# The last level of the block inverses in a hybrid decoder layer: 64 by 64 products in quarters of the TensorE array, in bundles of eight, in place of full operands with zeros

## The chip, the cores and the metric

The kernel runs on one core of a Trainium2 chip. The metric is the device time of one execution in microseconds (us). The kernel before took 1600.16 us (median of three runs, 1599.25 to 1602.24). One execution was also recorded by the hardware profiler; that one took 1599.81 us, and its span from the first to the last instruction is 1597.8 us. The engines are named as the profile names them: PE is TensorE's matmul side and PEld its weight loads, DVE is VectorE, ACT is ScalarE, POOL is GpSimd and SP is SyncE, which here only issues transfers.

## The reference

One decoder layer over 1024 positions of width 2048, followed by a final RMSNorm. An input projection feeds three groups of heads: a chunked spatial gating, a gated DeltaNet of 8 heads, and a cross-attention into 256 memory tokens. Their gated outputs go through one output projection. What the change touches is the inverse inside the DeltaNet, which the reference computes chunk by chunk with a triangular solve:

```python
    a = jnp.where(strict, jnp.einsum('bhnid,bhnjd->bhnij', kb, k) * decay, 0.0)
    eye = jnp.eye(C, dtype=f32)
    T = lax.linalg.triangular_solve(a + eye, jnp.broadcast_to(eye, a.shape),
                                    left_side=True, lower=True, unit_diagonal=True)
    value = jnp.einsum('bhnij,bhnjd->bhnid', T, vb)
    k_cumdecay = jnp.einsum('bhnij,bhnjd->bhnid', T, kb * jnp.exp(g_cum)[..., None])
```

## The kernel before

**The large products.** The input and output projections take most of the time. They are float32 products made of three TensorE products each: every operand is split into a high part and the rest (`ahi`, `alo`, `whi`, `wlo`, also `zh`, `zl`), and `triple` multiplies high by high, high by low and low by high. `seven` runs a block scheme with seven products per pair of column blocks (a pass of Strassen's kind), in sub-products with a 128 by 128 stationary operand and 512 moving columns. These appear in the profile as `acc<-ahi,whi 128*128 128x512` and the like; below they are called the main products.

**The DeltaNet beside them.** It works on chunks of 128 positions, for two heads and 512 positions at a time: eight chunk matrices, in the free dimension of one tile. `front` makes the products of keys and queries (through `qk`, whose `to_tokens` transposes eight blocks in a row), `inverse` inverts the 32 by 32 diagonal blocks on DVE, `levels` makes the inverse of each 128 by 128 matrix out of these, `values` prepares the values, and `back` runs the recurrence (`scan_step`) and the output (`heads_out`, again with eight transposes in a row). `backs` calls `front_late`, `levels`, `values` and `back` eight times in all, each for a pair of heads and a half of the sequence; in the profiled execution these calls lie between 720 and 1100 us.

**`levels` in steps.** Tile `gt` holds the eight matrices (views `ge`, `go`: even and odd chunks), `tblk` (`t`, `te`, `to`) the blocks of the inverse, `ut` (`u`, `ue`, `uo`) its transpose, which is the result. The diagonal blocks are fetched by transfers on POOL's queue. The first level goes from 32 to 64 with products of 32 by 32 in separate sub-arrays (`32*32` in the profile): a bundle of 16 products, copies to `y1` by ACT, a bundle of 24 products, copies by ACT. The last level goes from 64 to 128 and needs two products per chunk, each 64 by 64 by 64. In the kernel before, two chunks share one full operand: the block of the even chunk lies in `ge[0:64, :, 64:128]`, that of the odd chunk was copied by a transfer to `ge[64:128, :, 0:64]`, so that both stand on the counter-diagonal of a 128 by 128 stationary operand, and two memsets on DVE set its diagonal quarters to zero. One matmul with 64 moving columns then gives the product of the even chunk in output partitions 64 to 127 and that of the odd chunk in 0 to 63. There are four such matmuls for the eight chunks (`dn<-tblk,gt 128x64` in the profile), then two copies by ACT to the diagonally placed tile `z` (which is `y2`, set to zero once by POOL at the start), then four more matmuls (`dn<-ut,y 128x64`) and two copies to `ut`. A float32 matmul stands in the profile as two records of weights and two of products, so each group of four is eight records.

**What sets the order.** Nothing is issued as the code is read. `Plan.add` records every operation with its dependencies, `Plan.issue` plans all engines with costs in nanoseconds (`price`) and then issues everything in the order of the planned times. Of the operations that could start on an engine the one with the lowest `rank` goes first; main products have rank 9, so whatever else PE can do goes between them. An operation of PE that waits for another engine is planned at least `SLACK` (600 ns) after the planned end of what it waits for, within `levels` 800 ns more (`R.slow`). Operations recorded under `together()` become one bundle: they wait for everything that any of them needs and stand next to each other. After a bundle of more than eight operations (`len(head.tail) > 7`) the plan adds `SWITCH` (250 ns) to PE's clock. Matmuls outside a bundle are planned one by one, so other work can come between them. A float32 matmul is priced in `price` like this:

```python
            passes = 1 if ins[0].dtype == F32R else 2 if name == "transpose" else 4
            o.cost = max(13.3 + n / 2.4 * passes, 222.0 if passes == 4 else 110.0) if out.shape[0] == P else max(30.0, n / 2.4 * passes * out.shape[0] / P)
```

All instructions bear the profile's line L300, where the plan issues them, so they are told apart by their tiles.

Of the kernel before, what the change touches and what calls it, by code (L numbers as in the profile page):

```python
# [17 lines left out]
P = 128  # L18
# [42 lines left out]
class Plan:  # L61
# [27 lines left out]
    @contextmanager  # L89
    def rank(self, cls):  # L90
        old, self.cls = self.cls, cls
        yield
        self.cls = old
# [135 lines left out]
    def issue(self):  # L229
        free = dict.fromkeys(self.SEEN, 0.0)  # L230
        soon = {e: [] for e in free}
        now = {e: [] for e in free}
        held = {"dve": 0.0, "pool": 0.0}
        dma = 0.0
        beside = dict.fromkeys(free, 0.0)
        table = "exp"
        for o in self.ops:
            if o.n == 0 and o.lead is o:
                heapq.heappush(soon[o.eng], (0.0, o.idx))
        left = len(self.ops)  # L240
        while left:
            best = None
            for e in free:
                if now[e]:
                    t = free[e]
                elif soon[e]:
                    t = max(free[e], soon[e][0][0])
                else:
                    continue
                if best is None or t < best[0]:  # L250
                    best = (t, e)
            t, e = best
            while soon[e] and soon[e][0][0] <= t:
                i = heapq.heappop(soon[e])[1]
                heapq.heappush(now[e], (self.ops[i].cls, i))
            if e == "act":
                other = [(c + self.STAY * (self.ops[i].table not in (None, table)), i, c) for c, i in now[e]]
                _, i, c = min(other)
                now[e].remove((c, i))
                heapq.heapify(now[e])  # L260
                head = self.ops[i]
            else:
                head = self.ops[heapq.heappop(now[e])[1]]
            for o in (head, *head.tail):
                t = max(t, free[e])
                if o.table not in (None, table):
                    t, table = t + self.TABLE_LOAD, o.table
                o.at = t
                left -= 1
                if o.lock:  # L270
                    t = max(t, held["pool" if e == "dve" else "dve"])
                end = t + o.cost
                if o.lock:
                    held[e] = end
                free[e] = end - min(self.OVERLAP[e], 0.5 * o.cost)
                done = end + o.lat
                if o.moves:
                    dma = max(dma, end) + o.moves
                    beside[e] = max(beside[e], end) + 2 * o.moves
                    done = (dma if e == "sp" else max(dma, beside[e])) + self.DMA_FIXED + o.lat  # L280
                for s in o.succ:
                    if s.eng != e or o.moves:
                        when = done + self.SEEN[s.eng] + (self.SLACK if s.eng == "pe" else 0.0)
                    elif e == "pe":
                        when = free[e]
                    else:
                        when = end + 34.0
                    if o.moves or s.eng == "pe" != e:
                        when += s.late
                    if o.moves and s.eng == "pe":  # L290
                        when += o.land
                    s.ready = max(s.ready, when)
                    s.n -= 1
                    if s.n == 0:
                        heapq.heappush(soon[s.eng], (s.ready, s.idx))
            if len(head.tail) > 7:
                free[e] += self.SWITCH
        self.ops.sort(key=lambda o: (o.at, o.idx))
        for o in self.ops:
            o.fn(*o.args, **o.kw)  # L300
# [3 lines left out]
def kernel(  # L304
# [28 lines left out]
    R = Plan(nc)  # L333
    V, S, G, PE, Q = R.dve, R.act, R.pool, R.pe, R.sp
    rank, behind = R.rank, R.behind

    def C(shape, name, dt=F32):
        return sb.tile(list(shape), dt, name=name, tag=name)[:]
# [65 lines left out]
    ring = {t: Slots(t, 4, [P, HT]) for t in ("kT", "qT", "vs", "kd", "ai")}  # L404
# [19 lines left out]
    def tpb():  # L424
        turn["tp"] += 1
        return acc[2 + turn["tp"] % 2]
# [284 lines left out]
    tblk = C([P, 2 * NT, 64], "tblk")  # L711
# [81 lines left out]
    y2 = C([P, 2 * NT, 64], "y2")  # L793
# [240 lines left out]
    def levels(gt, tdr, udr):  # L1034


        NB = 2 * NT
# [7 lines left out]
        ut = ring["ut"]().rearrange("p (h t i) -> p h t i", h=2, i=P)  # L1045
        t, u = tblk, ut.rearrange("p h t i -> p (h t) i")
# [21 lines left out]
        d = work()  # L1068
# [6 lines left out]
        for b in (0, 64):  # L1075
            with rank(1):
                S.copy(y1[b + 32 : b + 64], d32[b + 32 : b + 64])
        with rank(1):
            V.memset(ge[0:64, :, 0:64], 0.0)
            V.memset(ge[64:P, :, 64:P], 0.0)  # L1080
        du = work()
        d32 = du[:, 0 : NB * 32].rearrange("p (c m) -> p c m", m=32)
        de, do = twos(d32)
        with R.together():
            for c in range(NB):
                for b in (0, 64):
                    PE.matmul(d32[b : b + 32, c], y1[b + 32 : b + 64, c], u[b + 32 : b + 64, c, b + 32 : b + 64],
                              start=True, stop=True)
                b = c % 2 * 64 + 32
# [9 lines left out]
                S.copy(u[b : b + 32, :, b + 32 : b + 64], d32[b : b + 32])  # L1099
        z = y2.rearrange("p (q e) m -> p q (e m)", e=2)  # L1100
        d = work()[:, 0 : NB * 32].rearrange("p (q m) -> p q m", m=64)
        for q in range(NB // 2):
            PE.matmul(d[:, q], ge[:, q], te[:, q], start=True, stop=True)
        with rank(1):
            S.copy(z[64:P, :, 0:64], d[64:P])
        with rank(1):
            S.copy(z[0:64, :, 64:P], d[0:64])
        d = work()[:, 0 : NB * 32].rearrange("p (q m) -> p q m", m=64)
        for q in range(NB // 2):
            PE.matmul(d[:, q], z[:, q], ue[:, q, 64:P], start=True, stop=True)  # L1110
        with rank(1):
            S.copy(ue[0:64, :, 64:P], d[0:64])
        with rank(1):
# [134 lines left out]
    a = tpb()  # L1248
# [29 lines left out]
    a = tpb()  # L1278
# [216 lines left out]
    def backs(ps, inv):  # L1495
        for hf in range(2):
            for p in ps:
                state = front_late(p, hf, inv[hf * 2 + p % 2])
                ut = levels(state[2], *state[-1])
                values(*state)  # L1500
                back(*state, ut)
# [9 lines left out]
    with rank(2.6):  # L1511
        gdrs += [front(1, hf) for hf in range(2)]
        early_inv = inverse([gdrs[i] for i in (0, 2, 1, 3)], "early", 1.9)
    for u in (y2, tblk, *ring["ut"].bufs):
        G.memset(u, 0.0)
    blocks(0, to_conv(0), to_conv(1))
    with rank(2.6):
# [313 lines left out]
```

## Time and profile before

| | |
|---|---|
| runs, median (lowest to highest) | 1600.16 us (1599.25 to 1602.24) |
| profiled execution, own time | 1599.81 us |
| its span, first to last instruction | 1597.8 us |
| granted TensorE clock | 0.999 |
| instructions | 26025 |

The span is cut into stages by looking at which tiles PE works on: up to some 110 us the memory's keys and values and the first half's rows, from there to about 1320 us the projections with the three groups of heads beside them, and then the output projection to the end. Matmuls overlap: a record of 128x512 lasts 0.39 us, but such records start every 0.227 us when they follow each other, so what something costs on PE is read from the starts of the rows around it and not from its busy time.

### The profile page before, as it was taken

Reading aid. Unit: us, or ns where it says so; the run is one execution under the profiler, and the core shown is the slowest. Engines: PE = TensorE matmul, PEld = TensorE weight load, DVE = VectorE, ACT = ScalarE, POOL = GpSimd, SP = SyncE. Lnnn points to the kernel's source line nnn. Section 1 sums busy time; section 2 is a strip of 40 time slices with the busy share of each in tenths; the row PEclk is TensorE's granted clock in tenths of the full one; section 3 lists DMA queues with packets and bytes.
Section 4 is the critical chain, followed back from the end, with each engine's and each line's share of the span. In section 5 each row is a group of like instructions: output and inputs, shape, how many; then the busy total and the mean of one; then the engine's idle time right before and its main releaser. Section 6 shows DMA issues by size and latency. Waiting matters only on the chain.

```text
span 1597.8 us, 26025 instructions
## 1 busy us (share of the span) xinstructions
PE 1582.5 (99%) x8580; PEld 1332.5 (83%) x8580; DVE 1314.9 (82%) x2157; ACT 1040.0 (65%) x2184; POOL 278.6 (17%) x456
## 2 busy tenths in 40 slices
PE   9999999999999999999999999999999999999997
PEld 8878888888888888888888888888888888888886
DVE  6879899869899999998988776867778788778776
ACT  7767648747755788976666667676566874344355
POOL 0101202211411412324342233032000000000001
PEclk9999999999999999999999999999999999999999
DMA  9987997897689868997789875788878879688746
GB/s 340 300 246 206 355 337 229 273 333 249 191 272 339 277 219 295 323 315 242 239 271 341 257 260 178 252 305 279 288 244 260 263 250 335 201 281 279 228 146 241
DMA packets 272744, 428.93 MB, mean 268 GB/s; under 512 B 30633, under 2 KB 97762, under 8 KB 272610
## 3 DMA queue, kind: packets, MB, share of 16 engines
q1 hardware_dynamic: 251138, 371.02, 70.9%
q0 software_dynamic: 20864, 55.20, 10.4%
q8 instruction: 67, 1.10, 0.3%
q10 hardware_dynamic: 608, 1.06, 0.2%
q14 instruction: 67, 0.55, 0.1%
HBM read 339.58 MB, written 87.06 MB: 267 GB/s over the span
## 4 chain that ended last, share of the span: by engine, by line
PE 94%; DMA 2%; ACT 1%; DVE 1%; issue 1%; SPq 0%; POOLq 0%; POOL 0%; ACTq 0%; DVEq 0%
PE acc L300 73%; PE dn L300 22%; DMA qT<-in_x_dram 0%; DMA h0d<-tn 0%; ACT whi L300 0%; DMA wraw<-in_w_in_dram 0%; DMA kvd<-vs 0%; DMA y<-h0d 0%; DMA wraw<-in_w_mem_kv_dram 0%; ACT jk L300 0%; SPq L300 0%; ACT tn L300 0%; DVE wlo L300 0%; ACT ahi L300 0%; DVE kT L300 0%
## 5 line engine op out<-in xcount | busy, mean ns | idle before, releaser
L300 PE MATMUL acc<-ahi,whi 128*128 128x512 f32 (+1 forms) x1488 | 513.4, 392 | 2.3 <-ACT ahi L300 1.1
L300 PE MATMUL acc<-ahi,wlo 128*128 128x512 f32 (+1 forms) x1040 | 404.8, 391 | 0.2 <-DVE wlo L300 0.2
L300 PEld LDWEIGHTS acc<-ahi,whi 128*128 128x128 f32 x1488 | 278.1, 188 | 57.0 <-ACT ahi L300 1.3
L300 PE MATMUL acc<-alo,whi 128*128 128x512 f32 (+1 forms) x592 | 229.2, 387 | 0.0
L300 PEld LDWEIGHTS acc<-ahi,wlo 128*128 128x128 f32 x1040 | 195.5, 188 | 37.2 <-DVE wlo L300 0.6
L300 ACT CAST ahi<-raws 128x1024 fp32r<-128x1024 f32 x148 | 155.4, 1050 | 64.0 <-PE acc L300 27.7
L300 PE MATMUL acc<-ahi,zh 128*128 128x512 f32 x448 | 176.5, 394 | 0.0
L300 PE MATMUL acc<-alo,zh 128*128 128x512 f32 x448 | 176.3, 394 | 0.0
L300 PE MATMUL acc<-ahi,zl 128*128 128x512 f32 x448 | 176.3, 394 | 0.0
L300 ACT CAST whi<-wraw 128x1024 fp32r<-128x1024 f32 (+1 forms) x116 | 108.0, 932 | 94.4 <-PE acc L300 75.6
L300 DVE TENSOR_TENSOR wlo<-wraw,whi 128x1024 fp32r<-128x1024 f32 (+1 forms) x116 | 124.2, 1073 | 38.0 <-ACT whi L300 34.4
L300 PEld LDWEIGHTS acc<-alo,whi 128*128 128x128 f32 x592 | 111.4, 188 | 20.8
L300 POOL TENSOR_TENSOR small<-small,mhalf 128x1 f32<-128x1 f32 x26 | 17.3, 672 | 525.0 <-DVE small L300 525.0
L300 DVE TENSOR_TENSOR alo<-raws,ahi 128x1024 fp32r<-128x1024 f32 x74 | 90.3, 1220 | 19.0 <-ACT ahi L300 18.4
L300 ACT CAST ahi<-y 128x1024 fp32r<-128x1024 f32 x74 | 77.7, 1049 | 40.3 <-PE dn L300 19.2
L300 DVE TENSOR_TENSOR alo<-y,ahi 128x1024 fp32r<-128x1024 f32 x74 | 90.3, 1220 | 16.1 <-ACT ahi L300 15.9
L300 DVE TENSOR_TENSOR ahi<-raws,ahi 128x1024 fp32r<-128x1024 f32 x74 | 90.4, 1222 | 15.1 <-ACT ahi L300 14.5
L300 PEld LDWEIGHTS acc<-alo,zh 128*128 128x128 f32 x448 | 84.2, 188 | 16.3
L300 PEld LDWEIGHTS acc<-ahi,zl 128*128 128x128 f32 x448 | 84.2, 188 | 16.1
L300 PEld LDWEIGHTS acc<-ahi,zh 128*128 128x128 f32 x448 | 84.2, 188 | 16.0
L300 PE MATMUL dn<-whi,ahi 128*128 128x512 f32 x224 | 77.1, 389 | 0.0
L300 PE MATMUL acc<-whi,ahi 128*128 128x512 f32 x216 | 74.9, 392 | 0.0
(464 smaller groups left out, 3451.4 us busy)
## 6 DMA issues: line engine op xcount, KB each, us to landing
wraw<-in_w_in_dram SPq DMA_DIRECT2D x224, 256.0 KB, 4.4
raws<-sa SPq DMA_DIRECT2D x128, 256.0 KB, 4.4
y<-in_w_in_dram SPq DMA_DIRECT2D x96, 256.0 KB, 4.1
y<-sa SPq DMA_DIRECT2D x64, 256.0 KB, 4.2
wraw<-in_w_out_dram SPq DMA_DIRECT2D x64, 256.0 KB, 4.4
raws<-h0d SPq DMA_DIRECT2D x62, 256.0 KB, 5.3
raws<-sd SPq DMA_DIRECT2D x44, 256.0 KB, 2.9
pd<-y SPq DMA_DIRECT2D x40, 256.0 KB, 5.2
```

Source lines behind the costliest of these rows:

```text
L300: o.fn(*o.args, **o.kw)
```

## The change

The last level's products are made one chunk at a time, each in a quarter of the array: 64 rows of the stationary operand by 64 columns. Each product of two chunks becomes two, one from partitions 0 to 63 into output partitions 64 to 127 and one the other way round. The eight of one step are a bundle. Since nothing reads the diagonal quarters any more, the two memsets of `ge` and the memset of `y2` go. In the plan the threshold for `SWITCH` goes from more than eight operations to eight, which takes in the new bundles and also the two calls of `to_tokens` with eight transposes (in `qk` and in `heads_out`).

```diff
@@ -293,7 +293,7 @@
                     s.n -= 1
                     if s.n == 0:
                         heapq.heappush(soon[s.eng], (s.ready, s.idx))
-            if len(head.tail) > 7:
+            if len(head.tail) > 6:
                 free[e] += self.SWITCH
         self.ops.sort(key=lambda o: (o.at, o.idx))
         for o in self.ops:
@@ -1075,9 +1075,6 @@
         for b in (0, 64):
             with rank(1):
                 S.copy(y1[b + 32 : b + 64], d32[b + 32 : b + 64])
-        with rank(1):
-            V.memset(ge[0:64, :, 0:64], 0.0)
-            V.memset(ge[64:P, :, 64:P], 0.0)
         du = work()
         d32 = du[:, 0 : NB * 32].rearrange("p (c m) -> p c m", m=32)
         de, do = twos(d32)
@@ -1099,15 +1096,20 @@
                 S.copy(u[b : b + 32, :, b + 32 : b + 64], d32[b : b + 32])
         z = y2.rearrange("p (q e) m -> p q (e m)", e=2)
         d = work()[:, 0 : NB * 32].rearrange("p (q m) -> p q m", m=64)
-        for q in range(NB // 2):
-            PE.matmul(d[:, q], ge[:, q], te[:, q], start=True, stop=True)
+        low, high = slice(0, 64), slice(64, P)
+        with R.together():
+            for q in range(NB // 2):
+                for a, b in ((low, high), (high, low)):
+                    PE.matmul(d[b, q], ge[a, q, b], te[a, q], start=True, stop=True)
         with rank(1):
             S.copy(z[64:P, :, 0:64], d[64:P])
         with rank(1):
             S.copy(z[0:64, :, 64:P], d[0:64])
         d = work()[:, 0 : NB * 32].rearrange("p (q m) -> p q m", m=64)
-        for q in range(NB // 2):
-            PE.matmul(d[:, q], z[:, q], ue[:, q, 64:P], start=True, stop=True)
+        with R.together():
+            for q in range(NB // 2):
+                for a, b in ((high, low), (low, high)):
+                    PE.matmul(d[b, q], z[a, q, b], ue[a, q, high], start=True, stop=True)
         with rank(1):
             S.copy(ue[0:64, :, 64:P], d[0:64])
         with rank(1):
@@ -1511,7 +1513,7 @@
     with rank(2.6):
         gdrs += [front(1, hf) for hf in range(2)]
         early_inv = inverse([gdrs[i] for i in (0, 2, 1, 3)], "early", 1.9)
-    for u in (y2, tblk, *ring["ut"].bufs):
+    for u in (tblk, *ring["ut"].bufs):
         G.memset(u, 0.0)
     blocks(0, to_conv(0), to_conv(1))
     with rank(2.6):
```

Because prices changed, the plan puts work in another order on every engine. On PE the first 756 rows of the order (a row is a run of equal instructions) and the last 1140 are as before; in between main products and DeltaNet work are shuffled against each other. Three places show what the prediction speaks of.

The first is PE at the first product of the last level, in the first call of `levels` (`gt_579`). Before:

```order
L300 MATMUL acc_108<-ahi_63,zh 128x512
L300 MATMUL acc_108<-alo_67,zh 128x512
L300 MATMUL dn_111<-tblk,gt_579 128x64 x4
L300 MATMUL acc_108<-ahi_63,zl 128x512
L300 MATMUL acc_106<-ahi_63,whi_74 128x512
```

And in the changed kernel:

```order
L300 MATMUL acc_105<-alo_67,whi_74 128x512
L300 MATMUL acc_105<-ahi_63,wlo_76 128x512
L300 MATMUL dn_111<-tblk,gt_579 64x64 x8
L300 MATMUL acc_105<-ahi_63,whi_74 128x512
L300 MATMUL acc_105<-alo_67,whi_74 128x512
```

Four matmuls of 128x64 have become eight of 64x64, between main products as before; the whole call stands earlier among the main products (other `acc` tiles around it).

The second is PE at the same product in the second call (`gt_590`), where the work of `scan_step` for the chunks of the first call (`steps`, `states`) is close by. Before:

```order
L300 MATMUL acc_107<-ahi_63,whi_74 128x512
L300 MATMUL dn_111<-tblk,gt_590 128x64 x2
L300 MATMUL dn_109<-steps,kd_582 128x128
L300 MATMUL dn_110<-steps,kd_587 128x128
L300 MATMUL dn_109<-states,qT_580 128x128
L300 MATMUL dn_109<-steps,ai_583 128x128
L300 MATMUL dn_110<-states,qT_585 128x128
L300 MATMUL dn_110<-steps,ai_588 128x128
L300 MATMUL dn_111<-tblk,gt_590 128x64 x2
L300 MATMUL acc_107<-alo_67,whi_74 128x512
```

And in the changed kernel:

```order
L300 MATMUL dn_109<-steps,ut_79 128x128
L300 MATMUL dn_110<-steps,ut_79 128x128
L300 MATMUL dn_111<-tblk,gt_590 64x64 x8
L300 MATMUL acc_105<-ahi_64,wlo_75 128x512
L300 MATMUL acc_105<-ahi_64,whi_73 128x512 x2
```

The group was split in two by the scan and is now whole. Before, four of the sixteen groups of all calls were split in this way.

The third is POOL's queue, where the loads for the second call stand (`tblk` its diagonal blocks, `gt_590` its gate matrices, then the copy within `gt_590` that fills the counter-diagonal). Before:

```order
L300 AFFINE_SELECT inv_576<-inv_576 128x1024
L300 DMA tblk<-tdrearly 32x8x32
L300 DMA tblk<-tdrearly 32x4x32 x3
L300 DMA kd_587<-late_1_2_218 128x512
L300 DMA ai_588<-late_1_3_219 128x512
L300 DMA gt_601<-gtd_0_280 128x1024
L300 DMA gt_590<-gtd_1_277 128x1024
L300 DMA gt_590<-gt_590 64x4x64
```

And in the changed kernel:

```order
L300 DMA tblk<-tdrearly 32x8x32
L300 DMA tblk<-tdrearly 32x4x32 x3
L300 DMA gt_601<-gtd_0_280 128x1024
L300 MEMSET inv_576 128x1024
L300 AFFINE_SELECT inv_576<-inv_576 128x1024
L300 DMA kd_587<-late_1_2_218 128x512
L300 DMA ai_588<-late_1_3_219 128x512
L300 DMA gt_590<-gtd_1_277 128x1024
L300 DMA gt_590<-gt_590 64x4x64
```

The memset and the select of `inv_576` now stand between the loads of `tblk` and that of `gt_590`.

## Prediction

> **What bounds the kernel now.** I read the busy times first, then a table of stages, then PE's waits.
>
> ```profile
> PE 1582.5 (99%) x8580; PEld 1332.5 (83%) x8580; DVE 1314.9 (82%) x2157; ACT 1040.0 (65%) x2184; POOL 278.6 (17%) x456
> 110.00:220.00 110.00, 109.49 (x632) 91.30 (x631) 96.72 (x184) 69.91 (x163) 16.04 (x28) 1.00 0.91 287
> 220.00:720.00 500.00, 500.00 (x2333) 417.60 (x2333) 447.96 (x708) 352.31 (x731) 120.50 (x191) 1.00 0.84 278
> 720.00:1100.00 380.00, 380.00 (x2670) 324.93 (x2669) 300.27 (x529) 257.92 (x611) 117.82 (x198) 1.00 0.80 260
> 158.10 0.50 PE L300 MATMUL acc<-ahi,whi 128*128 128x512 f32 x1 [0.33 <-ACT xr L300]
> 214.31 0.50 PE L300 MATMUL acc<-ahi,wlo 128*128 128x512 f32 x1 [0.18 <-DVE wlo L300]
> 1458.94 43.52 PE acc L300 x192
> ```
>
> In the stage table the columns are the window, its length, and the busy time of PE, PEld, DVE, ACT and POOL. PE is busy in all of 220 to 720 and of 720 to 1100 us, the stage of the eight calls of `levels`. Its idle time from 110 to 220 us is 110.00 - 109.49 = 0.51 us, which the two bracketed waits make up (0.33 and 0.18). So after 220 us PE waits for nobody: the span is the sum of what PE is given, and any other engine matters only if it makes PE wait. A row of the chain of waits gives the price of a main product: 43.52 / 192 = 0.2267 us from start to start.
>
> **What a group costs on PE.** From the timeline, with start and length in us: I take the start of the main product before a group and of the second one after it, and subtract two main intervals (0.454 us).
>
> ```profile
> 734.84 0.40 PE L300 MATMUL acc<-ahi,whi 128*128 128x512 f32 x1
> 735.08 1.00 PE L300 MATMUL dn<-ut,y 128*128 128x64 f32 x8
> 735.89 0.47 PE L300 MATMUL acc<-alo,whi 128*128 128x512 f32 x1
> 736.20 0.39 PE L300 MATMUL acc<-ahi,wlo 128*128 128x512 f32 x1
> ...
> 737.35 0.40 PE L300 MATMUL acc<-alo,whi 128*128 128x512 f32 x1
> 737.59 0.60 PE L300 MATMUL dn<-ident,tn 128*128 128x128 f32 x4
> 737.94 0.47 PE L300 MATMUL acc<-ahi,wlo 128*128 128x512 f32 x1
> 738.25 0.39 PE L300 MATMUL acc<-ahi,whi 128*128 128x512 f32 x1
> ```
>
> A product with zeros: 736.20 - 734.84 - 0.454 = 0.906 us for eight records, 0.113 each. Four transposes: 738.25 - 737.35 - 0.454 = 0.446 us, 0.112 each. Two groups of different length have the same price per record, so in the full array a group has no fee of its own. Joining the four split groups therefore brings nothing.
>
> ```profile
> 724.52 0.39 PE L300 MATMUL acc<-ahi,wlo 128*128 128x512 f32 x1
> 724.84 0.69 PE L300 MATMUL dn<-tblk,gt 32*32 32x32 f32 x32
> 725.46 0.50 PE L300 MATMUL acc<-ahi,zh 128*128 128x512 f32 x1
> 725.80 0.40 PE L300 MATMUL acc<-alo,zh 128*128 128x512 f32 x1
> L300 PE MATMUL dn<-tblk,gt 128*128 128x64 f32 x64 | 8.2, 266 | 0.0
> L300 PE MATMUL dn<-ut,y 128*128 128x64 f32 x64 | 8.2, 266 | 0.0
> L300 PE MATMUL dn<-tblk,gt 32*32 32x32 f32 x256 | 5.5, 192 | 0.0
> ```
>
> A bundle in sub-arrays costs 725.80 - 724.52 - 0.454 = 0.826 us. Its first and last starts are 0.69 - 0.19 = 0.50 us apart (the group's length less one record's, 192 ns). The other 0.33 us is the fee for going into sub-arrays and back: the bundle begins 0.32 us after the main product before it instead of 0.23, and main products come back at 0.12 and 0.34.
>
> **The change part by part.** *Removed:* 16 groups of eight records (the two rows of x64), 16 x 0.906 = 14.5 us of PE. *Added:* 16 bundles of 16 records in two quarters that share no row and no column. No row of before is a 64x64 tile, so I build the price from its neighbours. In the 32x32 bundle two sub-arrays take 16 records each in 0.50 us, which is 0.032 per record in its own sub-array. At 128 columns of weights the starts are (1.00 - 0.27) / 7 = 0.104 us apart. On the line between them 64 columns give 0.032 + (32 / 96) x 0.072 = 0.056. Eight records in each quarter, both at once, are 7 x 0.056 + 0.03 for the second quarter's start = 0.42 us. With the fee of 0.33 that is 0.75 us instead of 0.906: **0.15 us less per product, 16 x 0.15 = 2.4 us less** on PE.
>
> Bounds. If a 64-column record kept the 32-column pace, the inside would be 0.25 us, the product 0.58, the gain 16 x 0.33 = 5.2 us. If the two quarters did not overlap, the inside would be 15 x 0.056 = 0.84, the product 1.17, and the change would lose 16 x 0.26 = 4.2 us; with records at the full-width pace besides, 15 x 0.104 = 1.56, it would lose 16 x 0.98 = 15.7 us. I take the middle because overlap is visible wherever this kernel uses parts of the array:
>
> ```profile
> 112.58 0.62 PE L300 MATMUL acc<-kT,abw 128*32 128x128 f32 x16
> 113.02 0.62 PE L300 MATMUL acc<-qT,abw 128*32 128x128 f32 x16
> 113.45 0.62 PE L300 MATMUL acc<-kd,abw 128*32 128x128 f32 x16
> ```
>
> Sixteen records with four column strips in turn take 0.44 us, 0.027 each, where the same 128 moving columns in the full array cost 0.112: four at a time, with nothing lost.
>
> *DVE and POOL.* The memsets go:
>
> ```profile
> L300 DVE MEMSET gt<- 64x256 f32 x16 | 4.4, 272 | 1.9 <-PE dn L300 1.0
> L300 POOL MEMSET y<- 128x512 f32 x1 | 0.5, 527 | 13.1 <-DVE bt L300 13.1
> ```
>
> That is 4.4 us of a DVE which is busy 300.27 of 380 us, and 0.5 us of POOL. I cost both at nothing: PE's main products cover them, and PE waits for neither. Without that cover it would be at most 4.4 us more gain. No transfer is added or taken away. The copies by ACT behind the products keep their place and wait for one bundle instead of four matmuls, the same data.
>
> *The plan.* By the formula in `price` a step of the last level falls from 4 x 222 = 888 to 8 x 53 + 250 = 677 ns, close to the 0.906 and 0.75 us above; 24 bundles of eight transposes (16 in `qk`, 8 in `heads_out`) are planned 250 ns longer, which they do not take. Both shuffle the order from about here on:
>
> ```profile
> 163.44 0.39 PE L300 MATMUL acc<-ahi,whi 128*128 128x512 f32 x1
> 163.67 0.39 PE L300 MATMUL acc<-alo,whi 128*128 128x512 f32 x1
> ```
>
> These are PE's rows 756 and 757. Only the wait of 0.18 us at 214.31 lies behind them, so a new order has next to nothing to win in waits. It can win or lose in the pace beside small groups: from 736.20 to 737.35 (rows above) five main intervals take 1.15 us, 0.230 each, 3.3 ns over the undisturbed 0.2267.
>
> ```profile
> 720.00:1100.00 380.00, 302.04 (x1202) 1.00 0.80 260
> ```
>
> That row of the stage table is for tile `acc` alone: 1202 main products. All of them slower, or none, is 1202 x 3.3 ns = 4.0 us; I allow a third of that either way, 1.3 us, and take zero.
>
> **Sum.** 1599.81 - 2.4 = 1597.4 us for the profiled execution. The median of the runs is 0.35 us above it, so I predict 1597.8 us. This kernel's measurement tells about 0.2% (3.2 us) from no change; my forecast is 0.15%, just inside.
>
> **Rivals.**
>
> *Quarters that take turns.* Both quarters of a bundle write one PSUM bank, from different rows of the array. If that made them wait for each other, the loss is the 4.2 us worked out above: 1604.4 us, slower. It decides from the first bundle on, and the change would not do what it says. For it: no row shows 64x64 tiles. Against it: the 32x32 bundle of the row at 724.84 does the same, two row strips into one bank, and its 32 records are 0.016 us apart where one sub-array has 0.032. The Trainium skill, TensorEngine Tiling (Array Packing), section Restrictions and Gotchas, says that different row tiles cannot access the same PSUM bank simultaneously, which would be this rival; the 0.50 us of that bundle speak against it here. Chance 0.09.
>
> *A load that now comes too late.* The second call's first bundle needs `gt_590`:
>
> ```profile
> 735.26 1.78 POOL L300 DMA_DIRECT2D tblk<-tdrearly  x3
> 739.91 1.08 POOL L300 DMA_DIRECT2D gt<-gtd  x2
> 747.73 0.65 POOL L300 DMA_DIRECT2D gt<-gt  x1 [6.74 <-DMA gt<-gtd]
> 750.41 0.69 PE L300 MATMUL dn<-tblk,gt 32*32 32x32 f32 x32
> 731.08 0.97 POOL L300 MEMSET inv<- 128x1024 f32 x1
> 734.01 1.29 POOL L300 TENSOR_SCALAR_AFFINE_SELECT inv<-inv 128x1024 f32<-128x1024 f32 x1
> ```
>
> POOL's next instruction started at 747.73 when that load had landed, 2.7 us ahead of the bundle. In the new order the memset and the select, 0.97 + 1.29 = 2.3 us, stand ahead of the load. Behind a waiting bundle PE's whole queue stands still, so what is late beyond the margin is lost one for one. For it: POOL's queue is reordered for all eight calls, and the calls stand earlier among the main products. Against it: counted in the order, main products between the first product of the first call and this bundle go from 68 to 78, 10 x 0.227 = 2.3 us more room, as much as the memset and select take; and PE waited for no such load before. The price is a whole landing, 6.74 us, in one call: 1597.8 + 6.7 = 1604.5 us. Lateness of 2.4 us in all eats the gain, 5.6 us makes it slower by over 0.2%. Chance 0.17.
>
> *The quarters are quicker than the line says.* If 64 columns run nearer to the 32-column pace, the gain goes towards 5.2 us; half-way between 2.4 and 5.2 is 1596.4 us. For it: sub-arrays overlap without loss in the rows above. Against: twice the columns have to stream. Chance 0.12.
>
> **How the numbers follow.** The forecast has 0.62; its own range, from the third of 4.0 us and the error of the interpolation, is 1596.2 to 1599.4, and some three tenths of it (0.19) lie below 1597.0, where faster by over 0.2% begins. The quicker quarters (0.12) all lie there: faster 0.31. Turns (0.09) and three quarters of the late load (0.13) are slower: 0.22. The rest, 0.43 + 0.04, is within 0.2%: 0.47. The range goes from the full gain of the quicker case, 1595.0, to just over the two slower rivals, 1604.8; beyond it I leave later loads in several calls and full-width records.
>
> **What would show it.** In the changed profile a 64x64 group should read x16 with about 0.63 us (0.42 and one record of 0.2), begin 0.32 us after the main product before it, and be followed by 0.12 and 0.34. A group of over 1 us means turns. PE's waits after 220 us should stay empty; a bracket with a transfer at a `32*32` bundle would be the late load. DVE should lose 4.4 us with no effect on PE. I am wrong in sign if the 64x64 inside exceeds 0.58 us (0.906 - 0.33), and wrong in size if main products beside the calls change their pace by more than 1 ns on average.

## The result: 0.4% slower, and the profile after

The changed kernel took 1606.16 us (median of six runs, 1603.13 to 1608.3), the kernel before 1599.9 us beside it. The ratio is 1.0039, with a 95% interval of 1.0029 to 1.0049: 6.2 us slower, outside the predicted range of 1595.0 to 1604.8. The profiled execution of the changed kernel took 1603.54 us, 3.7 us more than that of before (1599.81); of the six runs it is the second fastest.

Busy times, and the stage table for the three windows shown of before and the start ahead of them:

```profile
PE 1584.2 (99%) x8708; PEld 1326.2 (83%) x8708; DVE 1305.8 (82%) x2141; ACT 1036.5 (65%) x2182; POOL 272.8 (17%) x455
...
0.00:110.00 110.00, 105.14 (x699) 92.48 (x703) 87.36 (x174) 85.49 (x185) 9.21 (x22) 1.00 0.97 308
110.00:220.00 110.00, 109.29 (x611) 90.44 (x604) 97.70 (x186) 69.21 (x161) 14.87 (x26) 1.00 0.92 288
220.00:720.00 500.00, 496.31 (x2373) 412.31 (x2373) 441.19 (x709) 346.92 (x731) 124.94 (x203) 1.00 0.82 277
720.00:1100.00 380.00, 380.00 (x2736) 320.23 (x2736) 289.82 (x504) 263.18 (x632) 116.51 (x195) 1.00 0.79 260
```

The stage with the new products, 720 to 1100 us, has no idle PE, as before. The stage ahead of it, in which no changed product runs, was full before (500.00 of 500) and now lacks 500 - 496.31 = 3.69 us.

**The quarters** did what they should. The first bundle in the timeline, and the two groups of instructions with their busy time and mean:

```profile
722.37 0.39 PE L300 MATMUL acc<-ahi,wlo 128*128 128x512 f32 x1
722.69 0.68 PE L300 MATMUL dn<-tblk,gt 64*64 64x64 f32 x16
723.30 0.50 PE L300 MATMUL acc<-ahi,whi 128*128 128x512 f32 x1
723.64 0.39 PE L300 MATMUL acc<-alo,whi 128*128 128x512 f32 x1
...
L300 PE MATMUL dn<-ut,y 64*64 64x64 f32 x128 | 5.5, 224 | 0.0
L300 PE MATMUL dn<-tblk,gt 64*64 64x64 f32 x128 | 5.4, 224 | 0.0
```

By the rule of the prediction a bundle costs 723.64 - 722.37 - 0.454 = 0.816 us, against 0.906 for the product with zeros: 0.09 us less, 16 x 0.09 = 1.4 us in all. First to last start are 0.68 - 0.22 = 0.46 us apart.

**The waits.** PE's waits from 220 to 720 us (tile, what it waited for, us in total, times, longest):

```profile
PE dn L300 <- DVE ai L300: 2.1, 2, 1.9
PE dn L300 <- DVE inv L300: 1.6, 2, 1.1
```

These are the 3.69 us: 0.25 us at 296 us, 1.07 at 518, 0.49 at 638 and 1.88 at 706. They stand in `qk` of `front`, 427 to 16 us ahead of the first changed product at 722.69 us. Two of the places in the timeline, DVE and PE:

```profile
513.11 1.22 DVE L300 TENSOR_TENSOR wlo<-wraw,whi 128x1024 fp32r<-128x1024 f32 x1
516.05 1.42 DVE L300 TENSOR_TENSOR qT<-qT,y 128x512 f32<-128x512 f32 x2 [1.73 <-DMA y<-in_w_in_dram]
517.38 0.68 DVE L300 TENSOR_TENSOR inv<-qT,inv 128x512 fp32r<-128x512 f32 x1
...
516.67 0.39 PE L300 MATMUL acc<-ahi,wlo 128*128 128x512 f32 x1
518.12 0.50 PE L300 MATMUL dn<-inv,inv 128*128 128x256 f32 x2 [1.07 <-DVE inv L300]
```

```profile
636.22 0.69 DVE L300 TENSOR_TENSOR wraw<-wraw,qT 128x512 f32<-128x512 f32 x1 [1.56 <-DMA wraw<-in_w_in_dram]
636.83 0.16 DVE L300 COPY lhs<-hs 128x8 f32<-128x8 f32 x1
636.90 0.68 DVE L300 TENSOR_TENSOR inv<-qT,inv 128x512 fp32r<-128x512 f32 x1
...
637.64 0.51 PE L300 MATMUL dn<-inv,inv 128*128 128x256 f32 x2 [0.49 <-DVE inv L300]
```

At 516 us DVE stands for 1.73 us in front of a difference of two weight blocks (`qT<-qT,y`, preparation of the large products), because the weight `y` is still on its way. Behind it in the same queue is `inv<-qT,inv`, the split of the queries that PE's next product reads. The bracket at PE names DVE; the cause, one instruction further back, is a transfer. At 636 us it is the same with `wraw`. The kernel before waits for such a weight at the same time, and its split (the ninth of 16 in both) comes later, behind two instructions that wait for nothing:

```profile
516.14 0.69 DVE L300 TENSOR_TENSOR qT<-qT,y 128x512 f32<-128x512 f32 x1 [1.19 <-DMA y<-in_w_in_dram]
...
525.42 1.22 DVE L300 TENSOR_TENSOR wlo<-y,whi 128x1024 fp32r<-128x1024 f32 x1
526.55 0.68 DVE L300 TENSOR_TENSOR inv<-qT,inv 128x512 fp32r<-128x512 f32 x1
```

The third place of the changed kernel:

```profile
703.91 1.22 DVE L300 TENSOR_TENSOR alo<-raws,ahi 128x1024 fp32r<-128x1024 f32 x1
705.05 0.69 DVE L300 TENSOR_TENSOR y<-y,kT 128x512 f32<-128x512 f32 x1
705.65 0.42 DVE L300 TENSOR_TENSOR gt<-dn,E 128x256 f32<-128x256 f32 x1
705.98 0.41 DVE L300 TENSOR_TENSOR ai<-dn,E 128x256 f32<-128x256 f32 x1
...
704.18 0.39 PE L300 MATMUL acc<-ahi,whi 128*128 128x512 f32 x1
706.45 0.39 PE L300 MATMUL dn<-inv 128*128 128x256 f32 x1 [1.88 <-DVE ai L300]
707.27 0.39 PE L300 MATMUL acc<-ahi,whi 128*128 128x512 f32 x1
707.50 0.39 PE L300 MATMUL acc<-ahi,wlo 128*128 128x512 f32 x1
707.73 0.83 PE L300 MATMUL acc<-ahi,whi 128*128 128x512 f32 x2
...
711.34 0.66 PE L300 MATMUL acc<-ahi,whi 128*128 128x512 f32 x2
711.84 0.39 PE L300 MATMUL acc<-ahi,wlo 128*128 128x512 f32 x1
```

```profile
708.00:711.40 3.40, 3.40 (x10) 2.63 (x9) 3.40 (x6) 0.00 (x0) 3.38 (x5) 0.50 0.72 234
```

Here DVE is busy without a gap, but `gt<-dn,E` and `ai<-dn,E`, which empty the bank that PE's next product writes, stand behind work for the large products. PE waits 1.88 us. Then its clock falls: the last row is the stage table from 708 to 711.4 us, with a granted clock of 0.50 in the third column from the end. From 707.73 to 711.84 there are eleven intervals of main products, (711.84 - 707.73) / 11 = 0.374 us each in place of 0.2267: **1.6 us more**, on top of the wait.

**The sum.** A wait costs more than its bracket, because the bracket begins at the modelled end of the matmul before it: from 704.18 to 706.45 the starts are 2.27 us apart, 2.04 more than a main interval, at a bracket of 1.88. So each wait costs 0.16 us besides, and the four of the stage 3.69 + 4 x 0.16 = 4.3 us. With -1.4 for the quarters, +1.6 for the half clock and +0.2 from 110 to 220 us (109.49 - 109.29 of idle time more, in two waits as before) that is +4.7 us, at the lower end of the interval of the ratio (0.29% to 0.49%, 4.6 to 7.8 us). It is the sum of one trace; the experiments show how much waits differ from one execution to the next. The profiled execution itself differs by 3.7 us only; its first 110 us, in which PE's order is that of before, had less idle time than in the profile of before:

```profile
0.00:110.00 110.00, 103.51 (x663) 90.92 (x664) 85.08 (x171) 83.70 (x181) 10.33 (x22) 1.00 0.96 304
```

This is the row of before: 105.14 - 103.51 = 1.6 us, and 4.7 - 1.6 = 3.1 is near the 3.7. The start varies from one execution to the next, whatever the kernel does later.

DVE's waits for weights from 220 to 720 us, changed kernel:

```profile
DVE wraw L300 <- DMA wraw<-in_w_in_dram: 6.5, 5, 1.6
DVE y L300 <- DMA y<-in_w_in_dram: 2.9, 3, 1.5
DVE kT L300 <- DMA wraw<-in_w_in_dram: 2.8, 3, 2.0
DVE kd L300 <- DMA wraw<-in_w_in_dram: 2.6, 1, 2.6
DVE qT L300 <- DMA y<-in_w_in_dram: 1.7, 1, 1.7
```

They come to 16.5 us; in the kernel before the same kinds of wait are there, but come to 7.8 us, none of them with work behind it that PE then waited for. Why the weights keep DVE waiting longer in the new order stays open.

### The profile page after: what moved, and what is told of

Its sections match the earlier page's. It is cut to its first block, busy times and chain, and to the rows that moved or that the text cites. A ratio compares the mean times of both kernels' runs of the same rounds, so it can differ in the third digit from the quotient of the medians.

```text
span 1601.7 us, 26283 instructions
## 1 busy us (share of the span) xinstructions
PE 1584.2 (99%) x8708; PEld 1326.2 (83%) x8708; DVE 1305.8 (82%) x2141; ACT 1036.5 (65%) x2182; POOL 272.8 (17%) x455
## 4 chain that ended last, share of the span: by engine, by line
PE 87%; DMA 8%; DVE 3%; ACT 1%; issue 1%; SPq 0%; POOLq 0%; POOL 0%; DVEq 0%; ACTq 0%
PE acc L300 66%; PE dn L300 20%; DMA wraw<-in_w_in_dram 2%; DMA y<-in_w_in_dram 1%; DMA wraw<-in_w_mem_kv_dram 1%; DVE wlo L300 1%; DMA gd<-y 1%; ACT whi L300 0%; DMA ut<-in_w_mem_kv_dram 0%; DMA qT<-in_x_dram 0%; DMA vs<-in_x_dram 0%; DMA pd<-y 0%; DMA states<-h0d 0%; DMA h0d<-tn 0%; DMA y<-sa 0%
```

## The experiments

The first theory: the quarters gain a little, and the loss is an order of DVE's queue in which work for the large products, waiting for weights or simply long, stands ahead of what PE needs; the order comes from the threshold for `SWITCH`. The rivals: the loss lies in the quarters themselves, in the new order of the eight calls, or in a new order of any kind. Four kernels separate the products from the order. Each was timed in five rounds beside the kernel before (1599.43 us).

**The order of before, with quarters.** In the kernel before each full product is issued as two quarters, where the plan still sees one product; the memsets stay.

```diff
-            PE.matmul(d[:, q], ge[:, q], te[:, q], start=True, stop=True)
+            PE.matmul(d[:, q], ge[:, q], te[:, q], start=True, stop=True).fn = quarters((low, high), (high, low))
...
-            PE.matmul(d[:, q], z[:, q], ue[:, q, 64:P], start=True, stop=True)
+            PE.matmul(d[:, q], z[:, q], ue[:, q, 64:P], start=True, stop=True).fn = quarters((high, low), (low, high))
```

> The order of the kernel before on every engine, row for row, memsets too; only when a full product with zeros is issued, its two quarters are issued in its place (a group split by the scan stays split, so four groups pay the fee for going into sub-arrays and back twice). Theory 'order' (the quarters gain, the loss is waits that the new order makes): per whole group 0.906 - 0.814 = 0.09 us less, 16 x 0.09 = 1.45 us, less four extra fees of 0.33 = 1.3 us: the span of before within 1.5 us, no wait of PE after 220 us but the 0.18 us at 214. Theory 'products' (the quarters themselves, or work around them, cost the time): ratio of 1.003 or more, 1604 us or above. My forecast's own price (0.75 us per product): 1.1 us less than before.

**The order of the change, with the full products.** The plan sees the changed kernel; at issue the first of two quarters issues the whole product and the second nothing, and the memsets are issued beside neighbouring work.

```diff
-                    PE.matmul(d[b, q], ge[a, q, b], te[a, q], start=True, stop=True)
+                    o = PE.matmul(d[b, q], ge[a, q, b], te[a, q], start=True, stop=True)
+                    o.fn = whole_op(a == low, d[:, q], ge[:, q], te[:, q])
```

> The changed kernel's order with the full products of before: where the first quarter of a pair would be issued the full product with zeros is, where the second would be nothing is; the memsets stand where they are needed without the plan knowing of them. Theory 'order': the waits of PE at 518, 638 and 706 us stay, and each of the 16 products costs 0.09 us more: 1.4 us over the changed kernel, 1607.5. Theory 'products': back to 1600.

**The threshold taken back,** in the changed kernel:

```diff
-            if len(head.tail) > 6:
+            if len(head.tail) > 7:
```

> The changed kernel with the threshold of the plan back at more than eight, so that neither the transposes nor the quarters are planned 250 ns longer. Theory 'threshold': this alone made the waits, and with it undone the time is that of before less 1.4 us, about 1598.5. Theory 'any new order': the order differs from both kernels, so PE has waits at other places than 518, 638 and 706 us, of 0 to 5 us in all; 1598 to 1605. Theory 'products': 1604 or above with no waits of PE.

**The threshold alone,** in the kernel before:

```diff
-            if len(head.tail) > 7:
+            if len(head.tail) > 6:
```

> The kernel before with nothing changed but the threshold. Theory 'threshold': as slow as the changed kernel or, without the gain of the quarters, 1.4 us slower: 1606 to 1608. Theory 'any new order': new waits at new places, 1600 to 1606. Theory 'products': the time of before, 1600.

| | median us | ratio to before (95%) | PE busy, 220 to 720 us |
|---|---|---|---|
| order of before, quarters | 1599.39 | 0.9999 (0.9990 to 1.0009) | 500.00 |
| order of the change, full products | 1607.1 | 1.0047 (1.0035 to 1.0059) | 494.04 |
| change, threshold back | 1598.76 | 0.9993 (0.9984 to 1.0001) | 500.00 |
| before, threshold alone | 1609.47 | 1.0062 (1.0049 to 1.0075) | 494.44 |

The time goes with the threshold, not with the products. One character in the planner's rule makes the kernel before 0.6% slower, with no product touched; taken back, it makes the changed kernel no slower than before. PE's waits in the kernel before with the threshold alone, from 220 to 720 us:

```profile
PE dn L300 <- DVE inv L300: 3.0, 2, 1.7
PE dn L300 <- DVE ai L300: 2.5, 2, 2.4
```

They are the same two kinds as in the changed kernel and longer, and the time is above the 1606 to 1608 us expected. With the threshold back that view has no row. The order of before with quarters has no wait in this stage either, but one of 0.54 us at 832 us that was not expected.

A trace is one execution, and waits differ between executions. The order of the change with full products runs PE, DVE and ACT in the changed kernel's order up to 716 us, and its trace has 500 - 494.04 = 5.96 us of waits in this stage where that of the changed kernel has 3.69. So a sum of waits from one trace is good to some 2 us, and the medians decide.

The stage table of the kernel with the threshold alone, after its wait of 1.7 us at 520 us and after that of 2.4 us at 710 us (the clock is the third column from the end):

```profile
520.00:526.00 6.00, 5.47 (x26) 4.65 (x27) 6.00 (x12) 0.01 (x1) 2.85 (x6) 1.00 0.68 187
711.10:714.50 3.40, 3.40 (x10) 2.62 (x10) 3.40 (x5) 0.00 (x0) 3.00 (x4) 0.51 0.70 225
```

The half clock follows the longer wait and not the shorter.

**Is it the order of DVE's queue?** The next experiment leaves the plan and all other queues as in the changed kernel and moves four DVE instructions, after the plan is made, ahead of the two or three in front of them that belong to the large products.

```diff
+        for o in sorted(self.first, key=lambda o: (o.at, o.idx)):
+            i = to = self.ops.index(o)
+            while i and self.ops[i - 1] not in needs.get(o, ()):
+                i -= 1
+                p = self.ops[i]
+                if p.eng == "dve":
+                    if p.cls != 2 and not (p.args and "lhs" in p.args[0].tensor.name) or p in self.first:
+                        break
+                    to = i
+            self.ops.remove(o)
+            self.ops.insert(to, o)
...
+            if i and (h, hf) in ((4, 0), (5, 1)):
+                R.first.append(R.ops[-1])
...
+            if t2 == 0 and (h, hf) == (7, 1):
+                R.first += R.ops[-2:]
```

> The changed kernel's plan and everything in it, but at issue four VectorE instructions of `qk` are moved ahead of the two or three VectorE instructions in front of them that belong to the large products (one product of `inv` near 518 us, one near 637 us, the pair `gt<-dn,E` and `ai<-dn,E` near 705 us); every other engine's queue stays as it is in the changed kernel. Theory of the blocked VectorE queue: TensorE's waits at 518, 637 and 706 us (1.07, 0.49 and 1.88 us) go to under 0.3 us in all, the half clock after the last one goes with them (1.6 us), TensorE's busy time from 220 to 720 us goes from 496.3 to over 499.5 of 500, and the median falls by 5 us or more below the changed kernel's 1606.2: 1598.5 to 1601.5, a ratio to before of 0.999 to 1.001. Rival, the new order of TensorE and of the transfers costs the time itself: the ratio stays at 1.003 to 1.005 (1604.2 to 1607.5), with waits in other places. Rival, the waits hide one another (TensorE would wait a little later for something else as late): each wait shrinks by less than half and the ratio stays over 1.002.

A second kernel moves only the last pair (the lines with `(4, 0), (5, 1)` left out):

> As the run with three places, but only the last pair (`gt<-dn,E` and `ai<-dn,E` near 705 us) is moved ahead of the two instructions of the large products before it (1.74 us by the rows of the changed kernel). Theory that the 1.88 us wait also sets off the half clock: the wait at 706 falls to 0.1 to 0.3 us and no stretch at half clock follows, so it gains 1.7 + 1.6 = 3.3 us on the changed kernel, 1602.0 to 1603.5, ratio 1.0015 to 1.0025; the waits at 518 (1.07 us) and 637 (0.49 us) stay. Rival, the half clock comes from something else than the wait (the load of all engines, a timer): it stays 3.4 us long near 708, and the gain is the wait alone, 1.7 us: about 1604.4, ratio 1.003.

Beside a kernel before of 1599.42 us the three places gave 1601.98 us, ratio 1.0016 (1.0007 to 1.0025), and the last pair alone 1603.06 us, ratio 1.0022 (1.0011 to 1.0033). Moving four of more than two thousand DVE instructions thus takes 1.0039 - 1.0016 = 0.23%, 3.7 us, off the changed kernel's excess of 6.2 us. With the three places, first the stage table, then PE and DVE at the first and the third:

```profile
220.00:720.00 500.00, 498.48 (x2405) 414.69 (x2403) 442.06 (x711) 351.24 (x739) 125.30 (x206) 1.00 0.83 278
708.00:711.40 3.40, 3.40 (x17) 2.82 (x16) 3.40 (x5) 1.21 (x2) 2.86 (x5) 1.00 0.91 263
```

```profile
514.43 0.69 DVE L316 TENSOR_TENSOR inv<-qT,inv 128x512 fp32r<-128x512 f32 x1 [0.24 <-ACT inv L316]
515.04 1.22 DVE L316 TENSOR_TENSOR wlo<-wraw,whi 128x1024 fp32r<-128x1024 f32 x1
516.99 1.48 DVE L316 TENSOR_TENSOR qT<-qT,y 128x512 f32<-128x512 f32 x2 [0.73 <-DMA y<-in_w_in_dram]
...
704.03 0.42 DVE L316 TENSOR_TENSOR gt<-dn,E 128x256 f32<-128x256 f32 x1
704.36 0.41 DVE L316 TENSOR_TENSOR ai<-dn,E 128x256 f32<-128x256 f32 x1
...
703.65 0.39 PE L316 MATMUL acc<-ahi,whi 128*128 128x512 f32 x1
704.83 0.39 PE L316 MATMUL dn<-inv 128*128 128x256 f32 x1 [0.79 <-DVE ai L316]
```

(The plan's line is 316 here, because lines were added above it.) The split now stands ahead of the wait for the weight: the DVE queue still waits there, PE no longer does. DVE's waits for weights in this stage stay at 16.1 us (16.5 in the changed kernel), while PE's go from 3.69 to 1.52 us: what counts is the work behind such a wait. At the third place the wait is 0.79 us in place of 1.88, and the clock in the window that had 0.50 is 1.00. In the stage 500 - 498.48 = 1.52 us of waits are left, where the expectation had under 0.3: the one of 0.79, one of 0.36 at 524 us that comes after the first moved place, and one of 0.38 at 296 us that was not touched. So the waits do not only vanish; a part of them comes back a little later, and the rival in which they hide one another is right to that extent. The ratio is above the forecast (0.999 to 1.001) for the same reason: 1.52 + 3 x 0.16 = 2.0 us for these waits, less the quarters' 1.4, and 0.4 us more each at 213 us (a wait of 0.6 us where before had 0.18) and at 730 us (one of 0.25 us, 380 - 379.75, with its 0.16) make 1.4 us over before, in its interval of 0.07% to 0.25%, 1.1 to 4.0 us. Of the 2.5 us of the excess that the moves leave, 1.4 are accounted for in this way, from one trace; no run takes them away.

With the last pair alone the clock stays full too; the wait is 0.52 us, where 0.1 to 0.3 was expected:

```profile
706.04 0.39 PE L316 MATMUL dn<-inv 128*128 128x256 f32 x1 [0.52 <-DVE ai L316]
```

The half clock goes when the wait of 1.88 us goes, and it does not come after the waits of 1.29 us (at 519 us) and 0.71 us (at 639 us) that this kernel keeps. So the wait set it off, and together they cost nearly twice the wait's own duration, 2.0 + 1.6 us.

**Which of the two costs of the threshold?** `SWITCH` after the quarters' bundles, but not after eight transposes:

```diff
-            if len(head.tail) > 6:
+            if len(head.tail) > 7 or len(head.tail) == 7 and head.args[0].shape[0] < P:
```

> The changed kernel with the 250 ns of `SWITCH` planned after the bundles of eight quarters, but not after the calls with eight transposes, as before. If the loss came from the planned cost of the transposes alone: no TensorE wait from 220 to 720 us (the plan there is as with the old threshold), ratio 0.998 to 1.000, 1597 to 1599.5, the quarters' gain of 1.4 us kept. Rival, that the planned cost of the quarters shuffles the later calls into waits: waits of TensorE in the 720 to 1100 us stretch of over 1 us, ratio over 1.001.

It took 1598.25 us, ratio 0.9992 (0.9983 to 1.0002). PE's busy time was 498.73 of 500 us from 220 to 720, where no wait was expected (0.92 us at 320 us and 0.35 at 529, which the same order did not have in the trace with the threshold back), and 380.00 of 380 after it. The 250 ns after the transposes made the loss; the shuffle of the eight calls by the quarters' planned cost made none that the median shows.

**Does any new order lose?** Two kernels change only a number of the plan in the kernel before.

```diff
-    SWITCH = 250.0
+    SWITCH = 300.0
```

> The kernel before with nothing changed but `SWITCH`, 300 ns in place of 250: the plan's estimate after long bundles, so only the order of the queues differs, from about 165 us on. Theory that a plan made anew has TensorE wait behind VectorE by chance, whatever was changed: one or two new waits of 0.5 to 2 us between 220 and 720 us, ratio to before 1.001 to 1.004 (1601 to 1606). Rival, that the loss belongs to the extra 250 ns after the transposes and not to any new order: busy time of TensorE from 220 to 720 us over 499.5 of 500, ratio 0.999 to 1.001.

```diff
-    SLACK = 600.0
+    SLACK = 620.0
```

> The kernel before with nothing changed but `SLACK`, 620 ns in place of 600: again only the order of the queues differs. The same two theories as for `SWITCH` at 300: new waits of 0.5 to 2 us between 220 and 720 us and ratio 1.001 to 1.004 if any new order draws such waits; over 499.5 of 500 us busy and ratio 0.999 to 1.001 if not.

`SWITCH` at 300 took 1599.15 us, ratio 0.9994 (0.9986 to 1.0003), PE busy 499.84 of 500; `SLACK` at 620 took 1600.68 us, ratio 1.0003 (0.9994 to 1.0012), PE busy 500.00. As tests they are unequal. Of PE's 2,422 rows from 110 to 722 us, 744 stand in another order in the changed kernel (they lie outside the longest sequence common to both), 264 with `SLACK` at 620 and 3 with `SWITCH` at 300, which hardly touches this stage. An order as far from that of before comes with the next edit (912 rows), and it does not lose. So the theory that any new order draws such waits falls: of the orders tried here only those with the 250 ns after the transposes lost, and not even all of these.

**A plan without that trap.** With `URGENT` at 1.95 the work of rank 2 on a loaded tile is planned 1 us later, so the plan should put less of it ahead of other work. The 250 ns after the transposes stay.

```diff
-    URGENT, LATE = 2.0, 1000.0
+    URGENT, LATE = 1.95, 1000.0
```

In the changed kernel, with its threshold:

> The changed kernel with one number of the plan changed: work of rank 2 that uses a transferred tile is planned 1 us later than it was (`URGENT` 1.95 in place of 2.0), so that VectorE's queue should have less of it standing in front of work that TensorE needs. If the theory of the blocked queue is right and the plan can be cured this way: TensorE's busy time from 220 to 720 us over 499 of 500, ratio 0.998 to 1.001. If the waits are a matter of chance in any order: waits of 1 to 4 us in other places, ratio 1.001 to 1.006. It also moves later work, so by itself it does not settle the cause.

The same kernel a second time, on another chip:

> The kernel with `URGENT` at 1.95 once more, unchanged, to see whether its lead over the kernel before (0.9988, interval 0.9979 to 0.9997) stands: ratio 0.998 to 0.9995 if it does, an interval around 1.000 if the first was chance.

And together with the threshold taken back:

> Quarters with the old threshold and `URGENT` at 1.95, the two settings that each left TensorE without waits from 220 to 720 us, now together. If the two gains are the same one (no waits, and the quarters' 1.4 us): ratio 0.998 to 0.9995, 1596 to 1598.5, and TensorE busy over 499.5 of 500. If a new order is a new draw: waits of 0.5 to 2 us somewhere, ratio 1.000 to 1.003.

The first gave 1597.04 us, ratio 0.9988 (0.9979 to 0.9997), the second 1598.24 us, ratio 0.9987 (0.9978 to 0.9996); PE was busy 500.00 and 499.20 of 500 us, two executions of the same kernel. The two settings together gave 1598.18 us, ratio 0.9991 (0.9982 to 1.0000), with PE busy 500.00 of 500 us, no better than either. So the change with `URGENT` at 1.95 is 0.1% faster than the kernel before in both tries, about 2 us, of which the quarters, by their price in the trace, explain 1.4.

## Why the prediction was wrong

**The step that failed** is the one on the plan: "Only the wait of 0.18 us at 214.31 lies behind them, so a new order has next to nothing to win in waits." That is true, and it is half of the question. In waits, a kernel whose PE never waits can only lose by a new order, and the loss was put at zero, plus or minus 1.3 us for the pace of main products. In the trace it was 4.3 us of waits and 1.6 us of half clock. The prediction had itself named the cause, 24 bundles planned 250 ns longer "which they do not take", and the place from which the order changes (163 us), and then looked for trouble only in the eight calls after 720 us.

**The rival of the late load** (0.17, 1604.5 us) has the right kind of mechanism, an instruction that waits for a transfer with PE's work behind it, and nearly the right price. The price is luck: it was one landing of 6.74 us, where the loss is made of four waits and a half clock, and at the costliest of them (1.88 us) DVE was busy and waited for no transfer. The place was wrong: not POOL's queue and `gt_590`, but DVE's queue, with weights in front of `qk`'s split. `gt_590` was not late, for PE waits for nothing from 720 to 1100 us.

**The quarters** were mis-sized, 0.75 us forecast and 0.816 measured, so 1.4 us gained where 2.4 stood. The inside took 0.46 us against 0.42, in all 16 bundles of the trace (the line between 32 and 128 columns is a little too low for 64), and the return to main products 723.30 - 722.69 - 0.46 = 0.15 us against 0.12. Sign and mechanism were right, and the rival of quarters that take turns is out: 16 records in 0.46 us are 0.031 apart, where one quarter alone at the interpolated pace, an estimate that no run times by itself, would need 0.056. The Trainium skill, TensorEngine Tiling (Array Packing), section Restrictions and Gotchas, says that different row tiles cannot access the same PSUM bank simultaneously; these 64x64 bundles write one bank from both halves of the rows, and the measured pace speaks against a loss from it here.

**Joining split groups** is worth nothing with full products and something with quarters, as each visit to sub-arrays pays its fee of about 0.33 us: in the order of before four of the sixteen groups are split and pay twice, 4 x 0.33 = 1.3 us, which by these sizes leaves 0.1 of the 1.4 us gained. The rows of that kernel agree: a split group costs 0.26 us more there than with full products, a whole one 0.085 less, and 4 x 0.26 is as much as 12 x 0.085. Its ratio of 0.9999 agrees too, but its interval of 3 us cannot tell it from the full gain.

**The memsets** at nothing: no result contradicts it. DVE lost 1314.9 - 1305.8 = 9.1 us of busy time in all, and PE shows no gain from it. **The pace of main products** at no change was right: from 720 to 1100 us, main products that follow each other directly start 0.2285 us apart before and 0.2286 after.

How it could have been seen: in the trace of before DVE waits 7.8 us for weights between 220 and 720 us. Each of these is a place where a change of a few positions in DVE's queue can put PE's next operand behind a transfer. The order of the change shows it without any time: at the place of 516 us two differences `qT<-qT,y` of freshly loaded weights stand right ahead of `inv<-qT,inv`, where before it was `alo` and `wlo`.

## What to carry to other kernels

Where one engine is busy throughout and never waits, a re-planned order has no wait to save and can only add some, so cost an edit to the planner's rules on its own, with the products unchanged, before the edit that it came with. Read the order of the *other* engines around each wait for a transfer: a waiting instruction that costs nothing today holds up whatever the new order puts behind it. And where PE is idle for nearly 2 us, in one wait or in two close together, price the half clock after it too: here it cost 1.6 us more.

## What was unexpected in the hardware

A single gap of 1.88 us in an otherwise full PE was followed, 1.5 us after its end, by 3.4 us at a granted clock of 0.50, and this cost 1.6 us. Gaps of 2.4 and 1.8 us, in the kernels with the threshold alone and with the full products in the new order, did the same at the same place in the program; gaps of 1.7 us in these two, and of 1.29 and 1.07 us elsewhere, had no such sequel.

It need not be one gap. In the second trace of the changed kernel with `URGENT` at 1.95, the half clock follows two waits, of 1.46 and 0.34 us, with matmuls between them:

```profile
70.62 0.38 PE L300 MATMUL acc<-ahi,whi 128*128 128x256 f32 x1 [1.46 <-ACT ahi L300]
71.35 0.83 PE L300 MATMUL dn<-ident,qT 128*128 128x128 f32 x4 [0.34 <-DVE alo L300]
...
71.70:75.10 3.40, 3.40 (x18) 3.27 (x17) 3.06 (x7) 2.79 (x7) 0.66 (x1) 0.50 0.86 217
```

In the 3.4 us before, PE was busy for 1.59 us, so idle for 1.81. Neither wait is as long as the gaps of 1.67 us that had no sequel. So the length of a single gap does not decide. The idle time within some 3.4 us fits these cases better: 1.81 us and more had the sequel, 1.67 us had not.

The Trainium skill, TensorE: Matmul & The Clock Gate, section Part 1: The HAM clock gate (the "warmup" mystery), puts the half rate after an idle window of about 3.4 us, in windows that run freely and do not start with the kernel. The 3.4 us at half clock agree with its window. That PE has to be idle for a whole window does not agree: PE was idle for 1.88 and 1.81 us here, with matmuls on both sides. Idle time as the profile models it is not the whole measure either: at the start of the order of before with quarters, PE was busy for 1.97 of the 3.4 us from 4.4 us on, so idle for 1.43, and the half clock followed. What exactly is counted, no run here shows.
